# Eight experts in one expert loop: four conditional places for the second block instead of six

## The chip, the cores and the metric

The kernel runs on one core of a Trainium2 chip. The metric is the device time of one execution in microseconds (us), as the median of the runs.

The engines are named as the profile names them: PE multiplies matrices, PEld loads its weights, DVE and ACT work element by element, POOL gathers rows, SP issues most of the transfers. Each engine takes its own instructions strictly in order.

## The reference

The reference is a two-layer encoder trunk. The part around the change is the mixture of experts in the second layer: 512 tokens, each sent to the two best of eight experts.

```
logits = hf @ w_router + b_router
top_logit, top_idx = lax.top_k(logits, 2);  gate = softmax(top_logit)
expert e:  y = (silu(x @ w1[e]) * (x @ w3[e])) @ w2[e]     # 1024 -> 1408 -> 1024
out[token] += gate * y
```

How many tokens an expert gets is known only on the chip.

## The kernel before

**Pieces.** An expert's weights come from HBM as 35 pieces of 128 rows in the order of `SEQ`. Pieces 0 to 7 and 8 to 15 are `w1` and `w3` for hidden columns 0 to 511 and 512 to 1023 (512 KB each). Pieces 16 to 19 are `w2` for the first of these chunks. Pieces 20 to 27 are `w1` and `w3` for the last 384 hidden columns (384 KB each). Pieces 28 to 31 and 32 to 34 are `w2` for the second and third chunk. In the text "piece 31" is the place of a piece in its expert.

**Buffers.** `fetch` (L1289) has SP issue the transfer of a piece into one of 18 raw buffers. `cut` (L1304, L1306) has ACT write the upper half of the number (`whi` or `r_hi`) and DVE the rest (`wlo` or `r_lo`) into a ring of 5; it runs 4 pieces ahead of PE.

**Two blocks of tokens.** `A` takes a piece for the expert's first 128 tokens (the first block): three products of the halves, six matmuls (L1353). `B` takes pieces for the tokens behind 128 (the second block), from the raw buffer, at fp32 (L1357). Whether there is a second block is decided at run time: `B` is a conditional place, with a body for up to 64 rows when the expert has over 160 tokens, a body for up to 32 rows when it has over 128, and nothing otherwise. Every engine with instructions in a body carries the compares and jumps of the place (L1505, L1508; L1502 for the last expert). In this run the first four experts skip their places, the fifth and seventh take the 32-row body and the sixth and eighth the 64-row body.

**Freeing.** A raw buffer is free when the cut and the second block are both done with it. So `refill` stands behind each place: passing the place releases the fetches of the pieces 18 further on, for all pieces that the place covers. In the skipped case PE passes the place without matmuls and signals all the same.

**Steps around a chunk.** `evac` computes silu times the other half (ACT L1368, DVE L1362 or L1369) and `turn` transposes the result for the down projection; for the second block ACT copies the transposed tile `gB` out of the bank `pub` (L1398), and the up projections of the second block write the same bank. Behind piece 28 and 29 `half_T` transposes the next expert's tokens (PE L1326, splits at L163 on ACT and DVE), and behind piece 30 `rows_T` transposes its second block (PE L1313) into the bank that the first `half_T` used. After the last expert `merge` (L1436) adds its output to the tokens.

**Order.** PE, ACT and DVE run in the order in which the code is written here. SP's instructions are placed by the scheduling layer; a body can hold the store of the second block's result on SP (`put`, L1411).

Of the kernel before, what the change touches and what calls it, by code (L numbers as in the profile page):

```python
# [25 lines left out]
NK = 8  # L26
# [3 lines left out]
NE = 8  # L30
# [14 lines left out]
def trunk(ctx, tc, I, out, dbg=None):  # L45
# [1053 lines left out]
    def moe(j, l, N, nxt):  # L1099
# [104 lines left out]
        def token_ids(es, b, ps, whole=True, make=True, count=True):  # L1204
            c = slice(b * 128, (b + 1) * 128)
            for e in es:
                oh_e = ohs[(2 * e + b) % 3]
                if make:
                    for t in range(NT):
                        ts(oh_e[:, t, :], iota256[:, c], posm[:, t, e:e + 1], None, op0=OP.is_equal)  # L1210
                for t in range(NT if count else 0):
                    done = mm(ps[:, (b * NE + e) * 2:(b * NE + e) * 2 + 2], oh_e[:, t, :], tk2[:, t, :],
                              start=(t == 0), stop=(t == NT - 1))
            if count:
                tm.append(done)
            if whole:
                return numbers(es, b, ps)

        def numbers(es, b, ps):
            q = slice(es[0], es[-1] + 1)  # L1220
            nc.vector.tensor_reduce(out=tif[:, b, q], in_=ps[:, 16 * b:16 * b + 16].rearrange("p (e c) -> p e c", c=2)[:, q],
                                    axis=AX.X, op=OP.add)
            return nc.vector.tensor_copy(TI[:, b, q], tif[:, b, q])

        def gather(xg, idx, src=hd):
            return nc.gpsimd.indirect_dma_start(out=xg, out_offset=None, in_=src,  # L1226
                                         in_offset=bass.IndirectOffsetOnAxis(ap=idx, axis=0))
# [30 lines left out]
        SEQ = []  # L1258
# [32 lines left out]
        def fetch_any(n, er=None):  # L1291
            if n < NW:
                fetch(n, er, nc.sync if er is None else nc.gpsimd)
            else:
                nc.sync.dma_start(out=raws[n % NRAW].rearrange("p (a b) -> p a b", a=2), in_=tail[n - NW])
# [12 lines left out]
        def rows_T(xg, he, banks):  # L1308
            n = xg.shape[0]
            per = 512 // n  # L1310
            for h in range(NK // per):
                for k in range(per):
                    done = nc.tensor.transpose(banks[h][:, k * n:(k + 1) * n],  # L1313
                                        xg[:, (per * h + k) * 128:(per * h + k + 1) * 128], ident[0:n, 0:n])
                p3 = banks[h].rearrange("p (k q) -> p k q", k=per)
                if n == 128:
                    split(p3, he[0][:, per * h:per * h + per, :], he[1][:, per * h:per * h + per, :])
                else:
                    act(he, p3, AF.Copy)
            return done  # L1320
# [8 lines left out]
        def quads(m, i):  # L1329
            return m == 32  # L1330
# [33 lines left out]
        def evac(i, m):  # L1364
            fw = FCH[i][1]
            if m == 128:
                src, gated = (tA[1] if i == 2 else tA[i])[:, :fw], tA[i % 2][:, :fw]
                act(src, pa_[2 * (i % 2)][:, :fw], AF.Silu)  # L1368
                (ordered if i == 2 else partial(tt, op=OP.mult))(out=gated, in0=src, in1=pa_[2 * (i % 2) + 1][:, :fw])  # L1369
            else:  # L1370
                n, w_ = (64, fw // 2) if quads(m, i) else (m, fw)
                act(tB[i % 2][64:64 + n, :w_], pub[0:n, :w_], AF.Silu)
                f = ordered if i == 2 and m == 64 else partial(tt, op=OP.mult)
                f(out=tB[i % 2][0:n, :w_], in0=tB[i % 2][64:64 + n, :w_], in1=pub[64:64 + n, :w_])
# [38 lines left out]
        def fold(m):  # L1413
            gather((xa, ye)[m % 2], G.slot[:, m % 2, m // 2:m // 2 + 1], yd)

        def add(m):
            t, i = m // 2, m % 2
            stt(X[t], (xa, ye)[i], G.gate[i][:, t:t + 1], X[t], op0=OP.mult, op1=OP.add)
# [21 lines left out]
        def expert(e, he, hb=None, total=NW + len(tail), base=None, er=None):  # L1440
            base = e * NP if base is None else base
            last = er is None and e == NE - 1
            state = {"a": 0, "b": 0, "cut": 0, "got": 0}

            def refill():
                while state["got"] < state["b" if er is None else "a"]:
                    n = base + state["got"] + NRAW
                    if n < total:
                        fetch_any(n, er)
                    state["got"] += 1  # L1450

            def hook(j):
                if e > 0 or er is not None:
                    return
                if j == 6:
                    rows_T(xb, heB[0], (pub,))
                    gather(xb, TI[0:64, 1, 1:2])
                if 3 <= j < 15:
                    i = j - 1
                    token_ids([i // 2 + 1], i % 2, (pd[0], pdb)[i % 2], whole=False, make=False)  # L1460
                if 2 <= j < 14:
                    token_ids([j // 2 + 1], j % 2, None, whole=False, count=False)
                if j == 14:
                    for b in range(2):
                        numbers(range(2, NE), b, (pd[0], pdb)[b])

            def A(*js):
                for j in js:
                    m = j // 2 - 8
                    if last and j % 2 == 0 and 0 <= m < 2 * NT:  # L1470
                        fold(m)
                    piece(base + j, 0, he)
                    hook(j)
                    state["a"] = j + 1
                    n = base + j + AHEAD
                    if n < total:
                        cut(n)
                        if er is None and 0 < e < 4:
                            next(rest, None)
                    if last and j % 2 and 0 < m <= 2 * NT:  # L1480
                        add(m - 1)
                    if SEQ[j][0] == "u" and SEQ[j][2] == NK - 1:
                        evac(SEQ[j][1], 128)
                    if er is not None:
                        refill()

            def B(lo, hi, before=None):
                if er is not None:
                    return

                def rest_of(m):
                    if before is not None:
                        turn(before, m)
                    for j in range(lo, hi):
                        piece(base + j, 1, hb, m)
                    if SEQ[hi - 1][0] == "u":
                        evac(SEQ[hi - 1][1], m)
                    if hi == NP and not last:
                        put(yd[NE * 128 + e * 64:NE * 128 + e * 64 + 64, :], m, nc.sync)

                if last:
                    with tc.If(cv[e] > 128):  # L1502
                        rest_of(64)
                else:
                    with tc.If(cv[e] > 160) as c:  # L1505
                        rest_of(64)
                    with c.Else():
                        with tc.If(cv[e] > 128):  # L1508
                            rest_of(32)
                state["b"] = hi  # L1510
                refill()

            A(*range(8))
            B(0, 8)
            A(8, 9, 10, 11)
            turn(0, 128)
            A(12, 13, 14, 15)
            B(8, 16, 0)
            A(16, 17, 18)
            turn(1, 128)  # L1520
            A(19)
            B(16, 20, 1)
            A(*range(20, 28))
            B(20, 28)
            A(28)
            if er is None:
                half_T(e + 1, 0)
            A(29)
            if er is None:
                half_T(e + 1, 1)  # L1530
            A(30)
            turn(2, 128)
            if er is None and e + 1 < NE:
                rows_T(xb, heB[(e + 1) % 2], (pa_[2],))
            A(31)
            ahead = er is None and e == NE - 2
            B(28, 35 if ahead else 32, 2)
            A(32, 33, 34)
            if er is None and not last:
                put(yd[e * 128:(e + 1) * 128, :], 128, nc.sync)  # L1540
            if not ahead:
                B(32, 35)
            if last:
                merge()

# [380 lines left out]
```

## Time and profile before

| | us |
|---|---|
| median of 3 runs | 1956.09 (1955.92 to 1959.73) |
| profiled execution, its own time | 1956.71 |
| its span, first to last instruction | 1955.2 |
| PE busy in the span | 1903.8 (97%) |

The times in the profile count from the first instruction. A matmul row of the timeline has the start of a pair and its modelled duration; since matmuls overlap, the distance between the starts of two rows is what a pair costs on PE (0.45 us for a pair of 512 columns, 0.35 for 384).

### The profile page before, as it was taken

To read this page: it belongs to the slowest core of one execution; us is meant where nothing else is said; L and a number is where in the kernel's file an instruction comes from. 1 tells how busy PE (TensorE), PEld (TensorE's weight loads), DVE (VectorE), ACT (ScalarE), POOL (GpSimd) and SP (SyncE) were. 2 spreads that over 40 slices of the span, in tenths; PEclk is the share of its full clock that TensorE was granted. 3 is DMA by queue.
4 is the path that set the end of the run, shared out by engine and by line. 5 is a ranking of instruction groups with operands and counts; after the bars stand their busy time and mean duration, and the time that the engine had idled before them with its cause. 6 is when DMAs were issued, how large, how long until landed. Compare 5 with 4: busy or idle time off the path is not lost. (4 is left out here: it accounts for less than half of the span.)

```text
span 1955.2 us, 27356 instructions
## 1 busy us (share of the span) xinstructions
PE 1903.8 (97%) x9954; PEld 1511.0 (77%) x9954; DVE 1186.8 (61%) x1859; ACT 908.1 (46%) x1349; POOL 332.7 (17%) x632
## 2 busy tenths in 40 slices
PE   7999999999999999999999999999999999999998
PEld 7787777888888888888787677887678877667666
DVE  5867565754333333345767565745899987666674
ACT  5535434333322222254534435333678876556553
POOL 2058220220000000001048320321100000000021
PEclk9999999999999999999999999999999999999999
DMA  5432223234433333432433232335699997756852
GB/s 168 120 116 87 77 91 128 84 95 168 137 97 94 101 97 97 119 91 62 135 114 98 66 92 85 126 96 212 236 370 368 371 357 272 264 202 251 326 160 99
DMA packets 95141, 309.39 MB, mean 158 GB/s; under 512 B 12609, under 2 KB 15681, under 8 KB 94978
## 3 DMA queue, kind: packets, MB, share of 16 engines
q1 hardware_dynamic: 89554, 290.06, 43.5%
q0 software_dynamic: 5280, 16.91, 2.5%
q8 instruction: 100, 1.64, 0.3%
q14 instruction: 63, 0.52, 0.1%
q10 hardware_dynamic: 144, 0.26, 0.0%
HBM read 283.59 MB, written 23.60 MB: 157 GB/s over the span
## 5 line engine op out<-in xcount | busy, mean ns | idle before, releaser
L137 ACT ACTIVATE whi<-wraw 128x1024 fp32r<-128x1024 f32 (+2 forms) x211 | 217.6, 1034 | 483.7 <-PE a L158 265.1
L139 DVE TENSOR_TENSOR wlo<-wraw,whi 128x1024 fp32r<-128x1024 f32 (+2 forms) x211 | 260.0, 1237 | 265.2 <-ACT whi L137 262.9
L157 PE MATMUL a<-hT_hi,whi 128*128 128x512 f32 (+3 forms) x1056 | 412.3, 391 | 1.4 <-ACT hT_hi L163 0.7
L158 PE MATMUL a<-hT_lo,whi 128*128 128x512 f32 (+3 forms) x1056 | 411.5, 390 | 0.8 <-DVE hT_lo L163 0.7
L159 PE MATMUL a<-hT_hi,wlo 128*128 128x512 f32 (+3 forms) x1056 | 411.6, 390 | 0.6 <-DVE wlo L139 0.6
L1306 DVE TENSOR_TENSOR wlo<-raw,whi 128x1024 fp32r<-128x1024 f32 (+1 forms) x198 | 227.8, 1159 | 45.1 <-ACT whi L1304 31.7
L158 PEld LDWEIGHTS a<-hT_lo,whi 128*128 128x128 f32 (+1 forms) x1056 | 197.1, 187 | 42.9 <-issue 2.8
L159 PEld LDWEIGHTS a<-hT_hi,wlo 128*128 128x128 f32 (+1 forms) x1056 | 197.1, 187 | 42.1 <-issue 3.2
L157 PEld LDWEIGHTS a<-hT_hi,whi 128*128 128x128 f32 (+1 forms) x1056 | 196.7, 187 | 42.5 <-issue 1.6
L1304 ACT ACTIVATE whi<-raw 128x1024 fp32r<-128x1024 f32 (+1 forms) x198 | 198.8, 1009 | 48.1 <-PE a L1353 30.4
L157 PE MATMUL a<-whi,hT_hi 128*128 128x256 f32 (+2 forms) x328 | 110.0, 335 | 1.1 <-ACT hT_hi L163 1.1
L159 PE MATMUL a<-whi,hT_lo 128*128 128x256 f32 (+2 forms) x328 | 109.0, 333 | 0.3
L158 PE MATMUL a<-wlo,hT_hi 128*128 128x256 f32 (+2 forms) x328 | 108.6, 331 | 0.0
L664 POOL TENSOR_TENSOR A<-A,t 128x512 f32<-128x512 f32 x48 | 76.4, 1625 | 179.2 <-DVE t L663 179.2
L1353 PE MATMUL a<-whi,heA_hi 128*128 128x512 f32 (+1 forms) x304 | 91.6, 382 | 4.7 <-PEq L1508 1.8
L1353 PE MATMUL a<-wlo,heA_hi 128*128 128x512 f32 (+1 forms) x304 | 88.7, 373 | 0.0
L1353 PE MATMUL a<-whi,heA_lo 128*128 128x512 f32 (+1 forms) x304 | 88.6, 372 | 0.0
L1353 PEld LDWEIGHTS a<-whi,heA_hi 128*128 128x128 f32 x304 | 54.2, 188 | 22.0 <-issue 8.3
L173 POOL TENSOR_SCALAR rs<-ss 128x1 f32<-128x1 f32 x8 | 2.3, 283 | 393.1 <-ACT sq L1773 392.7
L157 PEld LDWEIGHTS a<-whi,hT_hi 128*128 128x128 f32 x328 | 62.5, 191 | 7.0 <-ACT hT_hi L163 1.6
L159 PEld LDWEIGHTS a<-whi,hT_lo 128*128 128x128 f32 x328 | 62.5, 191 | 5.9 <-DVE hT_lo L163 0.9
L1226 POOL DMA_INDIRECT xa<-hd,TI x8 | 12.4, 1553 | 319.0 <-PE a L1326 310.8
(532 smaller groups left out, 3622.5 us busy)
## 6 DMA issues: line engine op xcount, KB each, us to landing
raw<-in_moe_w13a SPq DMA_DIRECT2D x113, 512.0 KB, 7.5
raw<-in_moe_w SPq DMA_DIRECT2D x74, 512.0 KB, 7.9
wraw<-in_w_gate SPq DMA_DIRECT2D x64, 512.0 KB, 3.6
wraw<-in_ffn_w SPq DMA_DIRECT2D x64, 512.0 KB, 3.6
raw<-in_moe_w13b SPq DMA_DIRECT2D x61, 384.0 KB, 7.2
wraw<-in_w_in_T SPq DMA_DIRECT2D x20, 512.0 KB, 3.3
wraw<-in_w_branch SPq DMA_DIRECT2D x16, 512.0 KB, 3.6
wraw<-in_w_o SPq DMA_DIRECT2D x16, 512.0 KB, 3.6
```

Source lines behind the costliest of these rows:

```text
L137: act(hi[:, :n], raw[:, :n], AF.Copy)
L139: tt(out=lo[:, :n], in0=raw[:, :n], in1=hi[:, :n].bitcast(F), op=OP.subtract)
L157: mm(o, a[0], b[0], start=start, stop=False)
L158: mm(o, a[0], b[1], start=False, stop=False)
L159: mm(o, a[1], b[0], start=False, stop=stop)
L173: gts(out=r[:, :n], in0=ss, scalar1=1.0 / dim, scalar2=EPS, op0=OP.mult, op1=OP.add)
L664: gtt(out=A[m], in0=A[m], in1=g[m], op=OP.add)
L1226: return nc.gpsimd.indirect_dma_start(out=xg, out_offset=None, in_=src, in_offset=bass.IndirectOffsetOnAxis(ap=idx, axis=0))
L1304: act(hi[:, :w], raw[:, :w], AF.Copy)
L1306: return tt(out=lo[:, :w], in0=raw[:, :w], in1=hi[:, :w].bitcast(F), op=OP.subtract)
L1353: mm(dst[x][:, :w_], st[sa][:, k, :], w[:, cs[x]], start=first and q == 0, stop=last and q == 2)
```

## The change

Pieces 8 to 19 of the second block run in one body, at the place that stood behind piece 19, and pieces 28 to 34 in one body behind piece 31 (the seventh expert had this already). The place behind piece 15 and the one behind piece 34 are gone. The transposes of the first and second chunk move with them: the first into the body of 8 to 19, the second into the body of 20 to 27. The evacuation of an up projection now stands in the middle of a body.

```diff
@@ -1493,8 +1493,8 @@
                     for j in range(lo, hi):
                         piece(base + j, 1, hb, m)
-                    if SEQ[hi - 1][0] == "u":
-                        evac(SEQ[hi - 1][1], m)
+                        if SEQ[j][0] == "u" and SEQ[j][2] == NK - 1:
+                            evac(SEQ[j][1], m)
                     if hi == NP and not last:
                         put(yd[NE * 128 + e * 64:NE * 128 + e * 64 + 64, :], m, nc.sync)
@@ -1514,14 +1514,12 @@
             B(0, 8)
             A(8, 9, 10, 11)
             turn(0, 128)
-            A(12, 13, 14, 15)
-            B(8, 16, 0)
-            A(16, 17, 18)
+            A(12, 13, 14, 15, 16, 17, 18)
             turn(1, 128)
             A(19)
-            B(16, 20, 1)
+            B(8, 20, 0)
             A(*range(20, 28))
-            B(20, 28)
+            B(20, 28, 1)
             A(28)
...
             A(31)
-            ahead = er is None and e == NE - 2
-            B(28, 35 if ahead else 32, 2)
+            B(28, 35, 2)
             A(32, 33, 34)
             if er is None and not last:
                 put(yd[e * 128:(e + 1) * 128, :], 128, nc.sync)
-            if not ahead:
-                B(32, 35)
             if last:
                 merge()
```

On SP, in the second expert, the place behind piece 15 stood in the middle of the fetches of pieces 26 to 34; now one place (behind piece 19) does what two did (rows cut from the difference; raw buffers by number, those shown carry `w2` pieces).

```order
 L1289 DMA raw_11661<-in_moe_w 128x1024
-L1505 COMPARE_AND_BRANCH
-L1505 UNCONDITIONAL_BRANCH
-L1508 COMPARE_AND_BRANCH
-L1508 UNCONDITIONAL_BRANCH x2
 L1289 DMA raw_11662<-in_moe_w 128x1024
 L1289 DMA raw_11663<-in_moe_w 128x1024
 L1289 DMA raw_11664<-in_moe_w 128x1024
 L1289 DMA raw_11665<-in_moe_w 128x1024
+L1505 COMPARE_AND_BRANCH
+L1505 UNCONDITIONAL_BRANCH
+L1508 COMPARE_AND_BRANCH
```

The order of the fetches among themselves is the same. The branch moved back on SP by four fetches; when a fetch may go is set by PE's signal for its raw buffer.

On PE, in the first expert, the place behind piece 27 (64-row body): `cst,ut` are the transposes of the second chunk into `pub` (tile `b`), the 64x384 rows are pieces 20 and 21, which write `pub` too.

```order
 L1353 MATMUL a<-r_hi,heA_lo 128x384 x2
 L1505 COMPARE_AND_BRANCH
+L1393 MATMUL b<-cst,ut 128x64 x4
 L1357 MATMUL b<-raw_11228,yh 64x384 x2
 L1357 MATMUL b<-raw_11229,yh 64x384 x2
```

The transposes moved from the body before the down projection into this one, directly ahead of the pieces that reuse their bank.

On PE, at the end of the last expert: the `a` and `b` rows at L1353 are its last first-block piece, L1502 its second-block place, and L1436 the first matmuls of `merge`.

```order
 L1353 MATMUL b<-wlo,gA_hi 128x512 x2
 L1353 MATMUL b<-whi,gA_lo 128x512 x2
-L1502 COMPARE_AND_BRANCH
-L1357 MATMUL b<-raw_11233,gB_11680 64x512 x2
-L1357 MATMUL b<-wraw,gB_11680 64x512 x4
-L1502 UNCONDITIONAL_BRANCH x2
 L1436 MATMUL a<-heA_hi,Sel 128x512
 L1436 MATMUL a<-heA_lo,Sel 128x512
```

The second block's last three pieces, which stood between the last first-block piece and `merge`, are now ahead of piece 32.

## Rows read from the trace of the kernel before

**Rows 1.** Fourth, fifth expert: us; PE, PEld, DVE, ACT, POOL busy (count); clock; DMA.

```profile
1547.28:1597.88 50.60, 49.70 (x238) 40.76 (x238) 45.28 (x46) 40.39 (x46) 2.98 (x2) 1.00 0.96 369
1597.88:1663.68 65.80, 65.43 (x524) 49.86 (x525) 48.05 (x50) 42.59 (x54) 2.54 (x2) 1.00 0.77 282
```

**Rows 2.** Timeline of PE, fourth expert: start, duration, instruction, tiles, shapes, count.

```profile
1569.57 0.61 PE L1353 MATMUL a<-whi,heA_lo 128*128 128x512 f32 x2
1570.34 0.71 PE L1353 MATMUL b<-whi,gA_hi 128*128 128x512 f32 x2
1570.88 0.62 PE L1353 MATMUL b<-wlo,gA_hi 128*128 128x512 f32 x2
1571.34 0.62 PE L1353 MATMUL b<-whi,gA_lo 128*128 128x512 f32 x2
...
1576.66 0.59 PE L1353 MATMUL a<-whi,heA_hi 128*128 128x384 f32 x2
...
1590.93 0.70 PE L1313 MATMUL a<-cst,xb 64*128 64x64 f32 x8
```

**Rows 3.** Sequencer instructions of line 1508: PE's compares, ns minimum, median and maximum.

```profile
L1508 PEldq COMPARE_BRANCH  x46: 65/207/1210, 1401.9 to 1804.1; - x46
```

**Rows 4.** Timeline of SP, fourth expert, fetches of pieces 26 to 32.

```profile
1570.31 0.80 SPq L1289 DMA_DIRECT2D raw<-in_moe_w13b  x2
...
1573.29 1.32 SPq L1289 DMA_DIRECT2D raw<-in_moe_w  x2
```

**Rows 5.** Issue to landing: fourth expert's pieces 28 and 31, third expert's 28.

```profile
raw<-in_moe_w SPq DMA_DIRECT2D x1, 512.0 KB, 5.8
...
raw<-in_moe_w SPq DMA_DIRECT2D x1, 512.0 KB, 7.5
...
wraw<-in_moe_w SPq DMA_DIRECT2D x1, 512.0 KB, 6.3
```

**Rows 6.** Timeline of ACT, fourth expert: silu, cut of piece 32, first token split.

```profile
1585.20 0.47 ACT L1368 ACTIVATE ut<-a 128x384 f32<-128x384 f32 x1
1585.88 1.06 ACT L1304 ACTIVATE r_hi<-raw 128x1024 fp32r<-128x1024 f32 x1 [0.20 <-ACTq L1508]
1587.49 0.60 ACT L163 ACTIVATE heA_hi<-a 128x512 fp32r<-128x512 f32 x1 [0.55 <-PE a L1326]
```

**Rows 7.** Timeline of DVE: the gated product, cut of piece 32, token split.

```profile
1586.76 0.61 DVE L1362 TENSOR_TENSOR ut<-ut,a 128x256 f32<-128x256 f32 x2
1587.60 1.23 DVE L1306 TENSOR_TENSOR r_lo<-raw,r_hi 128x1024 fp32r<-128x1024 f32 x1 [0.23 <-DVEq L1508]
1588.75 0.68 DVE L163 TENSOR_TENSOR heA_lo<-a,heA_hi 128x512 fp32r<-128x512 f32 x1
```

**Rows 8.** PE, fifth expert (32-row body): the two places around pieces 16 to 19.

```profile
1624.11 0.34 PE L1393 MATMUL b<-cst,ut 64*128 64x64 f32 x2
1624.81 1.93 PE L1357 MATMUL b<-raw,yh 128*32 128x256 f32 x32 [0.37 <-ACT gB L1398]
...
1633.99 0.62 PE L1353 MATMUL b<-whi,gA_lo 128*128 128x512 f32 x2
1634.55 0.33 PE L1393 MATMUL b<-cst,ut 64*128 64x64 f32 x2
1634.81 1.93 PE L1357 MATMUL b<-raw,gB 128*32 128x256 f32 x32
```

**Rows 9.** At the merge: ACT's splits, PE's second block and fifth matmul, DVE's split.

```profile
1887.48 1.08 ACT L163 ACTIVATE heA_hi<-b 128x512 fp32r<-128x512 f32 x2 [6.08 <-PE b L1353]
...
1888.50 1.89 PE L1357 MATMUL b<-wraw,gB 128*64 128x512 f32 x8
...
1892.15 0.40 PE L1436 MATMUL a<-heA_hi,Sel 128*128 128x512 f32 x1
...
1891.07 0.69 DVE L163 TENSOR_TENSOR heA_lo<-b,heA_hi 128x512 fp32r<-128x512 f32 x1 [1.67 <-ACT heA_hi L163]
```

**Rows 10.** Waits of SP, 1640 to 1815 us, its stores in a body.

```profile
SPq L1411 <- ACT yb L1409: 44.7, 3, 20.3
```

## The prediction

> **What bounds the kernel now.** I read the busy time by stretch first, one stretch per expert. In the fourth expert, which skips its second block, PE is busy for 49.70 of 50.60 us at a granted clock of 1.00, and at the same time the DMA engines are busy for 0.96 of it [rows 1]. So PE sets the pace there, and the transfers have almost nothing to spare. In the fifth, which takes its bodies, PE is busy for 65.43 of 65.80 us and the DMA share is 0.77 [rows 1]. The reader is to see two kinds of expert: four that skip, where any late transfer may show, and four that take a body, where PE alone counts.
>
> Then PE's timeline at a place [rows 2]. Pairs of matmuls start 0.46 us apart (1570.88 to 1571.34). Across the skipped place the distance is 0.77 (1569.57 to 1570.34), 0.31 more; the next pair takes 0.54 instead of 0.46. A skipped place costs PE 0.31 + 0.08 = 0.4 us.
>
> Last I followed SP's fetches beside PE. The fetch of piece 26, the first that the place behind piece 15 holds back, is issued at 1570.31 [rows 4], just as PE gets past that place (1570.34) [rows 2]. So passing the place is what releases it.
>
> **The change part by part.** *Places removed in the four skipping experts.* Two each, behind pieces 15 and 34, so 8 x 0.4 = 3.2 us less PE time. Nothing lies beside this, since PE is the busy engine: I count all of it.
>
> [...] The row of compares has 207 ns as its median on PE [rows 3], and the gap on PE is 0.31, so I stay with the gap.
>
> *The fetches of pieces 26 to 33.* These now wait for the place behind piece 19. In the fourth expert that is 1576.66 [rows 2] instead of 1570.34: 6.3 us later relative to PE's work. What covers that? Piece 31 is issued at 1573.29 [rows 4] and lands 7.5 us later [rows 5], at 1580.8, which is 10.5 us after the first fetch of its batch. If the batch restarts in the same manner, it lands at 1576.7 + 10.5 = 1587.2 on the old clock. Behind it ACT and DVE work in order, with durations from [rows 6, 7]:
>
> ACT cuts piece 31 (1.06, as for piece 32), to 1588.3; silu, 0.47, to 1588.8; cuts piece 32, to 1589.9; splits the first half of the next expert's tokens, 0.60, to 1590.5. DVE's part of piece 31 (1.23) ends at 1589.5, the gated product (0.61) at 1590.1, its part of piece 32 at 1591.4, its part of the token split (0.68) at 1592.1. PE's transposes at L1313 reuse the bank that this split reads; they start at 1590.93 today [rows 2], when the split is long over (1588.75 + 0.68 = 1589.4 [rows 7]). They would start 1.2 us later.
>
> So the 6.3 us are covered but for 1.2 us in the fourth expert. In the third, piece 28 lands 6.3 us after its issue, in the fourth 5.8 [rows 5], and piece 31 goes with it: about 1.7 us there. I take 1.5 us as the mean of the four skipping experts: 4 x 1.5 = 6.0 us more. The bounds: nothing, if the batch starts with 1.5 us less delay than today; 2.5 us each, if it starts 1 us worse than in the fourth expert and DVE has small extra work besides. With the saving that is -3.2 to +6.8 us for these experts, and +2.8 as the value taken. Can the transfers catch up, at a share of 0.96? The pause before piece 26 grows only in the first expert. After that the whole stream runs later by about this much and ends just as the next place is passed, so it costs once per expert and does not grow.
>
> *The four experts that take a body.* In the 32-row body of pieces 8 to 15, PE's transposes start at 1624.11 and the matmuls at 1624.81, since they write the bank that ACT is still copying from: 0.70 us. In the body of 16 to 19, which writes another bank, it is 0.26 [rows 8]. The second transpose now stands before pieces 20 to 27, which write the bank: a new wait of 0.44 us in each of four experts, more in a 64-row body, so I take 0.5, 2.0 in all. Against it, joining two bodies saves a switch: 0.1 on entering (0.56 from 1633.99 to 1634.55 instead of 0.46), and I take the same again for leaving and for the first pair behind it, 0.3. There are seven such switches (the seventh expert loses only one place): 2.1. The two cancel.
>
> The fetches in these experts have more cover: at a DMA share of 0.77 [rows 1] nothing queues long, and the bodies give PE work while they land. I put this at nothing; if the cover is gone it is the 1.2 us from above in the fifth, at most.
>
> *SP's store in a body.* SP waits up to 20.3 us for the result of the second block before it stores it [rows 10], and fetches stand queued behind. The store now stands earlier among the fetches, but the result is ready earlier too, by the first block's pieces 32 to 34 (3 x 1.4 = 4.1 us). Nothing, with 0 to 1 us each in two experts as bounds.
>
> *The merge.* In the last expert pieces 32 to 34 of the second block ran while ACT and DVE split the first block's result. ACT begins these splits at 1887.48, two take 1.08, and DVE's last takes 0.69 behind a third on ACT [rows 9]. Today PE reaches its fifth matmul of the merge at 1892.15, 4.7 us after 1887.48. With the second block already done, the chain is 1.08 + 0.5 on ACT, 0.1, 0.69 on DVE, then 0.4 on PE: 2.8. The three second-block pieces come earlier instead: twelve matmuls at 1.89 us for eight [rows 9] make 2.8, and I take 2.6, since the row's end overlaps what follows. 2.8 + 2.6 - 4.7 = 0.7 us more.
>
> **The sum.** -3.2 + 6.0 + 0.0 + 0.7 = +3.5 us. The profiled execution took 1956.71, so 1960.2; the median of the runs is 0.6 below it, so 1956.09 + 3.5 = 1959.6.
>
> **The rivals.** *A cheap restart, faster than before.* If the batch behind the later place lands 1.5 us sooner than its model, PE never waits at L1313, and 3.2 us are saved for 0.7: 1953.6. For it speaks that DMA might work off a longer run of fetches in a better stream; against it that today's restart, in much the same situation, took those 10.5 us for six pieces, 2.88 MB, which at the mean of 369 GB/s [rows 1] would take 7.8.
>
> *The transfers become the bound, clearly slower.* At a share of 0.96 [rows 1], a stream that runs 6 us later leaves little slack for cuts in the whole next expert. It decides as soon as piece 31 lands more than about 11.3 us after the first fetch: each us beyond that is a us on PE. At 2.5 us per expert: 4 x 2.5 - 3.2 + 0.7 = +7.5, 1963.6. For it speaks the fuller queue; against it that the queue empties just before each place.
>
> *The longer jump.* The longest of PE's 46 compares took 1.21 us against a median of 0.21 [rows 3]. The skipped body grows from eight pieces to twelve; a jump that stalls 1 us and is not hidden, once in each skipping expert, adds 4.0: 1963.6. The gaps on PE did not show that long compare as more than the usual 0.3 us, which speaks against. [...]
>
> *The places cost more than their gap.* If compares also delay ACT and DVE, 16 places less on each engine could be worth 5 us: 1951. The gap rows show no such thing.
>
> **How the numbers follow.** No change here means within 0.2%, 3.9 us, which is about what a measurement of this kernel can tell. The forecast, +3.5, gets 0.47; with 1.5 us either way it lies within the bound in two cases of three (0.32) and above it in one (0.15). The cheap restart gets 0.17, nearly all within. The transfers as the bound get 0.22 and the longer jump 0.07, both beyond. The places that cost more get 0.07, faster. Slower: 0.15 + 0.22 + 0.07 = 0.44; the same: 0.32 + 0.17 = 0.49; faster: 0.07. Range: from the cheap restart, 1953.5, to a little beyond the transfers as the bound, 1964.5. The likeliest case alone is 1958.1 to 1961.1.
>
> **What would show it.** Right, if the gaps behind pieces 15 and 34 are gone in the skipping experts, if the fetch of piece 26 goes out as PE passes the place behind piece 19, if PE stands before L1313 or a piece between 28 and 31 for about 1.5 us in each of them, waiting for DVE's split or a cut, if PE waits for `gB` in eight bodies instead of four, and if the merge shows about 1 us of wait. Wrong, if there is no wait at pieces 28 to 32, if the waits spread over the next expert's pieces, or if a gap at a place is longer than 0.4 us.

## The result: slower by 0.53%, more than forecast

The changed kernel takes 1968.24 us (median of 5 runs, 1965.85 to 1969.12), beside 1956.61 for the kernel before in the same session. The medians differ by 11.6 us. The ratio on record, over all runs, is 1.0053 with a 95% interval of 1.0042 to 1.0065, which is 10.4 us. The forecast was +3.5 us (1959.6) in a range up to 1964.5. The sign of the sum was right, its size was not, and the time lies outside the range.

### Where the time went

The start of each expert's first matmul pair in the two profiled executions (spans 1955.2 and 1967.6 us) splits the difference. The eighth ends at the fifth matmul of `merge`.

| expert | body | before, us | after, us | difference |
|---|---|---|---|---|
| first to fourth | skipped | 58.3, 50.6, 50.8, 50.6 | 59.1, 51.5, 52.2, 53.7 | +0.8, +0.9, +1.4, +3.1 |
| fifth | 32 rows | 65.8 | 67.1 | +1.3 |
| sixth | 64 rows | 80.4 | 80.2 | -0.3 |
| seventh | 32 rows | 67.6 | 72.7 | +5.1 |
| eighth | 64 rows, `merge` | 80.5 | 81.4 | +1.0 |

A row has the time from an expert's start to the next one's. The rows sum to +13.4 us. The first expert starts 1.0 us earlier, and what follows takes 63.0 us in both. The windows of the fourth, fifth and seventh expert of the changed kernel answer to [rows 1] (columns as there):

```profile
1549.41:1603.10 53.69, 50.97 (x239) 41.77 (x237) 44.98 (x47) 39.41 (x46) 2.87 (x2) 0.97 0.94 364
1603.10:1670.23 67.13, 64.81 (x525) 50.63 (x524) 46.87 (x49) 42.50 (x55) 2.55 (x2) 1.00 0.72 272
1750.40:1823.11 72.71, 66.63 (x525) 50.98 (x524) 48.61 (x50) 42.94 (x55) 0.00 (x0) 0.98 0.66 249
```

PE now stands idle in the fourth expert (50.97 busy of 53.69, where it was 49.70 of 50.60), and the granted clock, 1.00 before, is 0.97 and 0.98 over the fourth and the seventh. PE's waits from the first expert to the end, the largest sums (who waited for what, us in total, times, longest), name the places. Before:

```profile
PE a L1353 <- PEq L1508: 1.8, 5, 1.1
PE a L1353 <- DVEq L1730: 1.8, 1, 1.8
PE b L1357 <- ACT gB L1398: 1.7, 4, 0.5
```

After:

```profile
PE b L1357 <- ACT gB L1398: 6.5, 7, 3.9
PE a L1313 <- DVE heA_lo L163: 5.4, 4, 1.7
PE b L1357 <- issue: 2.0, 1, 2.0
PE a L1353 <- DVEq L1725: 1.8, 1, 1.8
PE a L1353 <- PEq L1508: 1.3, 2, 1.2
PE a L1436 <- DVE heA_lo L163: 0.7, 2, 0.5
PE a L1436 <- ACT heA_hi L163: 0.6, 1, 0.6
```

The second row of after is the wait that was forecast, once in each skipping expert. The first and the third are where the forecast fell short: `gB`, at most 0.5 us before and 0.37 in [rows 8], and forecast at 0.5 in each of four more bodies, costs 3.9 us once and 2.0 us once more. The latter is the "issue" row, in the fifth expert: the profile names no releaser, but PE starts as ACT's copy of `gB` ends.

```profile
1651.62 0.27 ACT L1398 ACTIVATE gB<-b 128x128 f32<-128x128 f32 x1
1651.98 1.34 PE L1357 MATMUL b<-raw,yh 128*32 128x192 f32 x27 [1.96 <-issue]
```

The 1.8 us at L1730 (L1725 after) are the start of the eighth expert, alike in both kernels.

The reader can follow the first kind of loss in the fourth expert, on PE (timeline: start, duration, instruction, idle time before it in brackets):

```profile
1592.76 0.55 PE L1393 MATMUL a<-cst,ut 128*128 128x128 f32 x3 [0.42 <-DVE ut L1362]
1595.01 0.71 PE L1313 MATMUL a<-cst,xb 64*128 64x64 f32 x8 [1.70 <-DVE heA_lo L163]
...
1596.80 1.06 PE L1353 MATMUL b<-whi,gA_lo 128*128 128x512 f32 x2
1598.01 1.19 PE L1353 MATMUL b<-r_hi,gA_hi 128*128 128x512 f32 x2
1599.00 1.05 PE L1353 MATMUL b<-r_lo,gA_hi 128*128 128x512 f32 x2
1599.85 0.69 PE L1353 MATMUL b<-r_hi,gA_lo 128*128 128x512 f32 x2
1600.38 0.62 PE L1353 MATMUL b<-whi,gA_hi 128*128 128x512 f32 x2
```

After the two waits the pairs come 0.99 and 0.85 us apart (1598.01 to 1599.85) instead of 0.46. The windows of the same stretch (granted clock third from the end) say why:

```profile
1592.50:1595.00 2.50, 0.55 (x3) 0.34 (x3) 2.27 (x5) 2.50 (x5) 0.68 (x1) 1.00 1.03 419
1595.00:1597.50 2.50, 2.50 (x14) 1.83 (x14) 2.50 (x3) 2.42 (x4) 0.90 (x1) 0.81 1.03 419
1597.50:1600.00 2.50, 2.35 (x6) 1.64 (x6) 2.50 (x4) 1.06 (x1) 0.00 (x0) 0.51 1.03 415
1600.00:1602.50 2.50, 2.50 (x13) 2.05 (x12) 1.33 (x2) 1.62 (x2) 0.00 (x0) 1.00 1.04 321
```

PE had worked 0.55 us of 2.50 at a granted clock of 1.00; then the clock fell to 0.81 and 0.51 over the next two stretches and came back to 1.00. From 1596.23 to 1600.38 five pairs took 4.15 us; at 0.454 each and 0.4 for the skipped place they would take 2.7. So the lower clock cost some 1.5 us there.

The second kind of loss, in the seventh expert, starts with idle transfers. The DMA row over 1770 to 1800 us (40 equal slices, busy share in tenths):

```profile
DMA  9999999721000000000000079975999999999999
```

SP's fetches (timeline, columns as for PE):

```profile
1786.40 0.80 SPq L1289 DMA_DIRECT2D raw<-in_moe_w13b  x2
1787.31 1.86 SPq L1289 DMA_DIRECT2D raw<-in_moe_w  x4
```

For some 10 us next to nothing is moved, since pieces 26 and up are fetched only once the joined body has used the buffers. ACT, which works in order, then takes the cuts as they land:

```profile
1794.34 1.06 ACT L1304 ACTIVATE whi<-raw 128x1024 fp32r<-128x1024 f32 x1 [1.60 <-DMA raw<-in_moe_w]
1795.56 1.06 ACT L1304 ACTIVATE whi<-raw 128x1024 fp32r<-128x1024 f32 x1 [0.16 <-DMA raw<-in_moe_w]
1798.36 1.06 ACT L1304 ACTIVATE whi<-raw 128x1024 fp32r<-128x1024 f32 x1 [1.74 <-DMA raw<-in_moe_w]
1799.58 1.06 ACT L1304 ACTIVATE whi<-raw 128x1024 fp32r<-128x1024 f32 x1 [0.16 <-DMA raw<-in_moe_w]
1800.54 0.47 ACT L1368 ACTIVATE ut<-a 128x384 f32<-128x384 f32 x1
1800.91 0.27 ACT L1398 ACTIVATE gB<-b 128x128 f32<-128x128 f32 x1
```

The copy of `gB` stands behind the cuts of pieces 28 to 31: ACT stands idle until 1798.36 for the third of these cuts, while the transposes that the copy takes (0.33 us from 1796.99, below) are done. PE, with pieces 20 to 27 in their buffers, waits for it because they write the bank `pub`:

```profile
1796.99 0.33 PE L1393 MATMUL b<-cst,ut 64*128 64x64 f32 x2
1801.23 4.49 PE L1357 MATMUL b<-raw,yh 128*32 128x192 f32 x64 [3.91 <-ACT gB L1398]
```

The same 64 matmuls took 2.81 us in the kernel before. The 4.49 here, 1.7 more, fall in a stretch of granted clock 0.66. Before (timeline) and after (window):

```profile
1791.50 2.81 PE L1357 MATMUL b<-raw,yh 128*32 128x192 f32 x64
1801.00:1806.00 5.00, 4.77 (x66) 3.19 (x67) 1.51 (x3) 0.36 (x3) 0.00 (x0) 0.66 0.65 238
```

### The profile page after: what moved, and what is told of

Same layout as the page of the kernel before. It is cut to its first block, busy times and chain, and to the rows that moved or that the text cites. A ratio compares the mean times of both kernels' runs of the same rounds, so it can differ in the third digit from the quotient of the medians.

```text
span 1967.6 us, 27167 instructions
## 1 busy us (share of the span) xinstructions
PE 1903.2 (97%) x9954; PEld 1514.1 (77%) x9954; DVE 1185.2 (60%) x1859; ACT 904.9 (46%) x1349; POOL 327.3 (17%) x632
## 5 line engine op out<-in xcount | busy, mean ns | idle before, releaser
L1353 PE MATMUL a<-whi,heA_hi 128*128 128x512 f32 (+1 forms) x304 | 90.9, 380 | 4.0 <-DVEq L1725 1.8
L1353 PE MATMUL a<-wlo,heA_hi 128*128 128x512 f32 (+1 forms) x304 | 88.6, 372 | 0.0
L1353 PE MATMUL a<-whi,heA_lo 128*128 128x512 f32 (+1 forms) x304 | 88.5, 372 | 0.0
L1353 PEld LDWEIGHTS a<-whi,heA_hi 128*128 128x128 f32 x304 | 54.6, 188 | 18.9 <-issue 6.8
L158 PEld LDWEIGHTS a<-wlo,hT_hi 128*128 128x128 f32 x328 | 62.5, 191 | 4.7
```

The lines of the kernel that those rows point to most:

```text
L158: mm(o, a[0], b[1], start=False, stop=False)
L1353: mm(dst[x][:, :w_], st[sa][:, k, :], w[:, cs[x]], start=first and q == 0, stop=last and q == 2)
```

## The experiments

The theory after the comparison: all of the loss comes from the later release of the fetches of pieces 26 to 34, by a late chain on ACT and DVE in the skipping experts, by `gB` queued behind late cuts in the experts with a 32-row body, and by the clock that falls after such waits. The rivals: the joined bodies or the moved transposes cost it by themselves, the last body carries it, or PE's pieces are late as such. Each kernel ran in 5 rounds beside the kernel before, except the last one told, which ran once. The ratios are those on record, over all runs of a kernel and of the kernel before in the same session; times by expert are of one profiled execution each.

**One half of the change each.** `only_28_34` is the kernel before with `B(28, 35, 2)` in all experts:

```diff
-            ahead = er is None and e == NE - 2
-            B(28, 35 if ahead else 32, 2)
+            B(28, 35, 2)
...
-            if not ahead:
-                B(32, 35)
```

> The kernel before with one half of the change: pieces 28 to 34 in one body in every expert; pieces 8 to 15 and 16 to 19 stay in two places. Theory (late release): the place behind piece 15 still releases the fetches of pieces 26 to 33, so nothing new is waited for. Four skipped places less at 0.4 us make -1.6, three joined bodies at 0.3 make -0.9, the merge costs +1.0: about -1.5, so 1955.1 us against 1956.6. Rival (the long last body or the merge carries the loss): 1962 or more.

1955.96 us, ratio 0.9991 (0.9982 to 1.000). The skipping experts two to four take 50.2 us each instead of 50.6 to 50.8, the eighth, with the merge, 81.4 instead of 80.5. A skipped place is worth its 0.4 us, and the joined last body brings no net loss, though the merge costs the eighth expert 0.9. `only_8_19` is the other half, the changed kernel with pieces 28 to 34 in two places as before:

> The changed kernel with pieces 28 to 32 and 32 to 34 in two places as before, so only pieces 8 to 19 are joined, behind piece 19. Theory (late release): all of the loss is here. Against the changed kernel the merge gives back 1.0 us and four skipped places and three switches cost 2.5: about 1969.5 us. Rival (the last body carries the loss): 1960 or less.

1971.38 us, ratio 1.0069 (1.0054 to 1.0085). The six runs lie between 1966.4 and 1974.5, so its distance to the changed kernel is not clear. All of the loss is in joining pieces 8 to 19 behind piece 19.

**The joined body at an earlier place.** `early_8_19`:

```diff
-            A(12, 13, 14, 15, 16, 17, 18)
+            A(12, 13, 14, 15)
+            B(8, 20, 0)
+            A(16, 17, 18)
             turn(1, 128)
             A(19)
-            B(8, 20, 0)
```

> The changed kernel with the one body of pieces 8 to 19 standing behind piece 15 instead of behind piece 19: as many places and bodies as in the changed kernel, but the fetches of pieces 26 and up are released as early as in the kernel before. Theory (late release): no wait for the token split at the transposes behind piece 30, no long wait for gB, no fall of the clock; eight skipped places less make -3.2, seven switches -2.1, four short gB waits +2.0, the merge +1.0: about -2.3, 1954.3 us. Rival (the joined body or the moved transposes cost it by themselves): like the changed kernel, 1966 to 1969.

1958.85 us, ratio 1.0010 (1.0001 to 1.0019). Of the changed kernel's 11.6 us nearly all are gone, with the same bodies: the wait at L1313 no longer shows, `gB` costs at most 0.5 us, and the clock is 1.00 in every expert. But it is no gain of 2.3 us either. A new wait stands right at the place, in the second expert (timeline of PE):

```profile
1468.52 0.61 PE L1353 MATMUL a<-whi,heA_lo 128*128 128x512 f32 x2
1470.43 0.70 PE L1353 MATMUL b<-whi,gA_hi 128*128 128x512 f32 x2 [1.30 <-PEq L1508]
```

PE's sequencer spent 4972 ns in one compare that began at 1465.30 (4635 ns at 1566.36 in the fourth). The matmul pair behind it could have started at 1469.1, 3.8 us after the compare began, so only the rest shows. In 1464 to 1472 us the DMA queue for instructions moved two blocks:

```profile
q8 instruction: 2, 0.03, 1.9%
```

The first of them was moved from 1467.95 to 1468.91, within the compare, which ended at 1470.27. This is the stall that the forecast's rival of the longer jump had in view. The changed kernel hides it: its longest compares in these experts are 1847 and 1197 ns, and only the second is at this place.

**The transposes of the second chunk back ahead of the late cuts.** `turn_back` is the changed kernel with

```diff
+                    if hi == 20:
+                        turn(1, m)
                     if hi == NP and not last:
...
-            B(20, 28, 1)
+            B(20, 28)
```

> The changed kernel with the second block's transposes of the second chunk moved to the end of the body of pieces 8 to 19, so that ACT copies gB before the late cuts of pieces 28 to 31 and not behind them; the fetches stay late. Theory (in the experts with a body the loss is gB's copy queued behind late cuts): the waits for gB go (2.0 us in the fifth expert, 3.9 and about 1.7 of lowered clock in the seventh, 0.5 each in the sixth and eighth), the waits of the skipping experts stay: 1959 to 1961 us. Rival (the pieces themselves are late for PE): the waits come back at the first block's pieces 28 to 31 in the fifth and seventh, 1966 to 1968.

1963.30 us, ratio 1.0025 (1.0014 to 1.0036), 2 us above the expected band. The experts with a body confirm the theory. The fifth and the seventh:

```profile
1604.99:1670.09 65.10, 64.73 (x526) 50.24 (x524) 46.70 (x50) 42.52 (x55) 2.53 (x2) 1.00 0.75 292
1749.68:1816.75 67.07, 64.90 (x526) 50.08 (x524) 48.63 (x50) 43.03 (x55) 0.00 (x0) 1.00 0.71 273
```

They take 2.0 and 5.6 us less than in the changed kernel and are 0.7 and 0.5 shorter than before [rows 1], although the fetch of piece 26 goes out nearly as late as in the changed kernel (35.6 us after the start of either expert; there 36.0, in the kernel before 29.3 and 29.4). So what cost them was the copy of `gB` behind late cuts on ACT, and a joined body by itself is a gain. The band was missed elsewhere: the skipping experts kept their waits at L1313 (5.2 us in four) and had 1.1 and 0.9 us of new waits for DVE beside them, one fell to a clock of 0.97 behind a wait of 1.50 us, and the 63.0 us behind the experts became 64.6. There the clock fell to half at 1897.7 (0.92 over the 64.6 us, where the changed kernel has 0.95 over its 63.0), behind two short waits in the merge (0.57 and 0.45 us), which the changed kernel has too (0.55 and 0.46) without a fall behind them.

**Another bank for the waiting transposes.** `turn_back_pub` changes one more word:

```diff
-                rows_T(xb, heB[(e + 1) % 2], (pa_[2],))
+                rows_T(xb, heB[(e + 1) % 2], (pub,))
```

> The kernel turn_back (changed kernel, second transposes back in the body of pieces 8 to 19) with the transposes of the next expert's second block (L1313) written into the bank pub instead of the bank that the token split still reads. Theory (the skipping experts lose only at that bank: the late split is waited for, PE's own pieces are not late): the four waits at L1313, 5.2 us, go, and no wait of that size takes their place: 1956 to 1958 us. Rival (the transfers are late as such): PE waits as long at the cuts of pieces 31 and 32, 1961 to 1964.

1961.63 us, ratio 1.0025 (1.0014 to 1.0036). My theory of the bank falls. The waits at L1313 are gone and others of nearly the same sum stand behind the next piece, at piece 32 (waits of PE in the skipping experts and the start of the fifth):

```profile
PE b L1353 <- DVE gA_lo L163: 2.6, 3, 0.9
PE b L1353 <- ACT gA_hi L163: 2.0, 2, 1.5
PE b L1353 <- DVE wlo L1306: 0.5, 2, 0.2
```

The rival had the size, though not the tile: PE waits for the split of `gA` for piece 32, which ACT and DVE reach late because the cuts ahead of it are late. The bank was only where the delay first surfaced.

**How late is too late.** `mid_8_19` puts the body behind piece 17, with the transposes at its end as in `turn_back` and the last expert's pieces 32 to 34 apart as before:

```diff
-            A(12, 13, 14, 15, 16, 17, 18)
+            A(12, 13, 14, 15, 16, 17)
+            B(8, 20, 0)
+            A(18)
...
-            B(28, 35, 2)
+            B(28, 32 if last else 35, 2)
...
             if last:
+                B(32, 35)
                 merge()
```

> The joined body of pieces 8 to 19 behind piece 17, between the two places tried: second transposes at its end, pieces 32 to 34 of the last expert apart as before. The fetches of pieces 26 and up are then released 2.8 us later than in the kernel before, not 6.3 us. Theory (6.3 us less a wait of 1.1 to 1.7 us says that some 4.8 us are covered, and the long compares on PE come from instruction fetches behind a full DMA queue): no wait at L1313, compares under 3 us, hence hidden; eight skipped places make -3.2, the joined bodies -2: about 1952 us. Rival 1 (the long jump itself costs 4 to 5 us as behind piece 15): 1954 to 1956. Rival 2 (any later release costs): waits at L1313 stay, 1956 or more.

1952.36 us, ratio 0.9971 (0.9962 to 0.9981): faster than both kernels, as forecast. No wait at L1313. The compares were not under 3 us, though: 3044 ns in the second expert, hidden, and 4688 ns in the fourth, where 1.1 us shows. That they come from fetches of instructions was a guess of mine, which no run shows. So rival 1 holds in part. The same kernel with the body behind piece 16 and behind piece 18:

> The kernel mid_8_19 with the joined body behind piece 16 instead of 17: fetches released 1.4 us later than in the kernel before. Theory (up to some 4.8 us of delay is covered): no wait at L1313, skipping experts at 49.8 us apart from compares, 1952 to 1953 us. Rival (an earlier release helps by itself): below 1951.

> The kernel mid_8_19 with the joined body behind piece 18: fetches released 4.2 us later than in the kernel before, 2.1 us earlier than in the changed kernel. Theory (some 4.8 us are covered, by the waits of 1.1 to 1.7 us out of 6.3): waits at L1313 under 0.3 us each, 1952 to 1954 us. Rival (the cost grows with each us of delay from the start): some 0.7 us in each skipping expert, 1955 to 1957.

Behind 16: 1952.59 us, ratio 0.9974 (0.9963 to 0.9985), experts two to four at 49.8 us each. Behind 18: 1953.13 us, ratio 0.9973 (0.9962 to 0.9984), but these experts take 50.3, 50.7 and 49.8 us. Two small waits are all that the list of waits shows there:

```profile
PE a L1393 <- DVE ut L1369: 0.6, 1, 0.6
PE a L1313 <- DVE heA_lo L163: 0.4, 1, 0.4
```

Both are in the third expert. A release 1.4 or 2.8 us later costs nothing, one of 4.2 us costs 0 to 0.9 us in an expert, one of 6.3 us costs the waits of the changed kernel. By these executions the cover, the delay that costs PE nothing, ends between 2.8 and 4.2 us, sooner than the 4.8 that I had expected. The times of the runs do not tell 2.8 from 4.2 (ratios 0.9971 and 0.9973).

**The jump.** `one_body` is `mid_8_19` with only the 64-row body at the place of pieces 8 to 19 in the first four experts:

```diff
-                if last:
+                if last or (lo == 8 and hi == 20 and e < 4):
                     with tc.If(cv[e] > 128):
```

> The kernel mid_8_19 in which the first four experts have only the 64-row body at the place of pieces 8 to 19 (one compare instead of two, half the instructions to jump over; they skip it in any case). Theory (the compares of 3.0 and 4.7 us at that place are jumps over a long stretch of instructions): compares under 2 us there, no gap of 1.1 us in the fourth expert, one compare less in four experts: 1950 to 1952 us. Rival (the long compares come from somewhere else, as from the transfers beside them): they stay at 3 us or more, 1951.5 to 1953.

1950.89 us, ratio 0.9958 (0.9944 to 0.9971), the lowest of all, though its interval overlaps with that of `mid_8_19`. The compares at that place take at most 0.35 us (one of 1219 ns is left, behind piece 31 and hidden), and the wait of 1.1 us is gone too:

```profile
1445.12:1494.95 49.83, 49.23 (x238) 40.92 (x237) 46.74 (x76) 41.35 (x48) 2.63 (x2) 1.00 0.97 376
1494.95:1544.77 49.82, 49.22 (x239) 40.93 (x238) 46.97 (x67) 41.12 (x47) 2.96 (x2) 1.00 0.95 376
1544.77:1594.58 49.81, 49.21 (x239) 40.91 (x237) 45.23 (x46) 40.22 (x46) 2.36 (x2) 1.00 0.96 373
```

With two bodies of twelve pieces to jump over, behind piece 15, 16 or 17, the compare took 3.0 to 5.0 us in the second and the fourth expert and at most 0.35 in the first and the third; with one body it is short in all four. The edit also takes out a compare and shifts the code behind it, so the length of the jump is not told apart from where the code falls. The DMA share of these experts (0.95 to 0.97) is that of `mid_8_19` (0.96 and 0.97), so a full stream of transfers does not make the long compare by itself. This form suits experts that skip; one with up to 32 rows would take the larger body, which no run shows.

**The merge.** `last_apart` is `only_28_34` with the last expert as before:

```diff
-            B(28, 35, 2)
+            B(28, 32 if last else 35, 2)
...
             if last:
+                B(32, 35)
                 merge()
```

> The kernel only_28_34 with pieces 28 to 32 and 32 to 34 of the last expert in two places as before. Theory (the merge is slower by 1 us because its splits on ACT and DVE have nothing beside them): the waits of the merge go, the last expert takes 80.5 us instead of 81.4, about 1 us less than only_28_34, so 1954.5 to 1955.5. Rival (it is the joined body): no difference to only_28_34.

1954.36 us, ratio 0.9988 (0.9979 to 0.9997). The waits for `heA_hi` and `heA_lo` in the merge (0.6 and 0.7 us) shrink to one of 0.2, and the last expert takes 80.5 us instead of 81.4. The intervals of the two kernels overlap, so the 0.9 us rest on the profiled executions.

**The clock by itself.** `stall` makes PE wait in the kernel before:

```diff
+            for _ in range({1: 2, 2: 5, 3: 9}.get(e, 0) if er is None else 0):
+                act(pa_[2], pa_[2], AF.Copy)
             if er is None and e + 1 < NE:
                 rows_T(xb, heB[(e + 1) % 2], (pa_[2],))
```

> The kernel before with extra copies on ACT, which PE has to wait for at the transposes behind piece 30: two copies in the second expert (PE idle about 1.3 us), five in the third (about 2.7), nine in the fourth (about 4.5). Theory (the granted clock falls after PE has stood idle long enough, and then costs by itself): the clock stays at 1.00 in the second expert and falls behind the wait in the fourth, where the next pairs take twice as long for some us, so the fourth loses some 2 us more than its wait. Rival (the falls seen in the changed kernel came from elsewhere): the clock stays at 1.00 in all three, each loses its wait alone.

One execution: 1975.6 us. The waits became longer than meant, 2.91, 3.52 and 5.98 us, so no expert had a short one. All three fell (second to fourth expert):

```profile
1446.53:1501.54 55.01, 51.20 (x238) 41.65 (x238) 47.83 (x78) 42.83 (x50) 1.85 (x2) 0.97 0.98 365
1501.54:1557.21 55.67, 51.14 (x238) 41.88 (x238) 47.29 (x65) 44.13 (x52) 2.72 (x2) 0.97 0.91 340
1557.21:1616.76 59.55, 52.68 (x238) 42.83 (x238) 45.30 (x46) 45.51 (x55) 2.73 (x2) 0.91 0.87 328
```

Against [rows 1] and the table above they lose 4.4, 4.9 and 9.0 us, that is 1.5, 1.4 and 3.0 more than the waits, and no other wait of theirs grew. That such a wait of PE brings the fall with it, and what it costs, is shown; from what length on is not.

## Why the prediction was wrong

**Right: the mechanism in the skipping experts.** The forecast said that fetch 26 goes out as PE passes the place behind piece 19 (it does in the fourth expert: 1578.28 on SP, 1578.31 on PE) and that PE then waits at L1313 for the split on DVE, 1.2 to 1.7 us in each, 6.0 in all. It waits 1.09, 1.33, 1.26 and 1.70 us, 5.4 in all. From the landing of piece 31 on, the chain took what was reckoned (1590.05, ACT's cut, to 1594.95, the split's end: 4.9 us, as forecast). The landing itself was later: ACT began the cut 11.1, 10.7, 11.1 and 11.8 us after the first fetch in the four experts, where 10.5 was reckoned. The saving of 0.4 us a place was right too (`only_28_34`).

**Mis-sized there.** These four experts were to lose 2.8 us and lost 6.2. The late chain also shows at other tiles (0.4 us twice before transposes, some of 0.2), about 1.5 us together; the fall of the clock in the fourth adds another 1.5. With 5.4 for the wait and -3.2 for the places that makes 5.2; the last 1.0 us is not accounted for. The sum of the prediction had no term for the clock.

**The step that failed** is "The fetches in these experts have more cover: ... I put this at nothing; if the cover is gone it is the 1.2 us from above in the fifth, at most." With the moved transposes, priced at 0.5 us each, they cost 2.0 us in the fifth and 3.9 in the seventh, and the clock 1.7 more: 7.6 us, where the sum had 1.0. The fifth to seventh expert together were forecast at nothing and lost 6.1, most of what the forecast missed. I had looked at the DMA share and at PE's own pieces, and both were indeed no problem. What I left out is the third in the chain: ACT holds the cuts of pieces 28 to 31 and `gB` in one queue, with the cuts first since they run four pieces ahead. I had priced the moved transposes at the copy alone, 0.5 us, without asking what stands ahead of the copy on its engine. It took both changes: with early fetches (`early_8_19`) the moved transposes cost 0.39 to 0.47 us each, as forecast, and with late fetches but the transposes back ahead of the cuts (`turn_back`) the 2.0 and 5.6 us are gone. The size in the seventh is partly chance: there ACT began the cut of piece 31 13.2 us after the first fetch, in `only_8_19`, with the same order, 11.8, and that wait was 2.5 us.

**Joined bodies are a gain.** I let seven switches (2.1) and the new waits (2.0) cancel. Without these waits the fifth and seventh expert are 0.7 and 0.5 us shorter than before (`turn_back`), so the switches were mis-sized little.

**The merge** was forecast at +0.7. The eighth expert takes 0.9 us more in `only_28_34`, with one switch saved that the forecast counts elsewhere at 0.3, so it was mis-sized by some 0.5; its waits are those of the chain behind [rows 9].

**The rivals.** Two of them had 1963.6, nearest in time. The transfers as the bound were to decide once piece 31 lands more than 11.3 us after the first fetch; the cut began past that in the fourth expert alone. The stream was full while it caught up (a share of 1.03 to 1.04 from 1592.5 to 1602.5), but `mid_8_19` moves the same pieces at 0.96 to 0.97 without such a wait, so what costs is the late release. The stall that the longer jump was to bring did come on this program (a compare of 4.97 us in `early_8_19`) and is hidden in the changed kernel; it takes 1.0 to 1.3 us of PE's time where nothing else delays PE. That the length of the jump makes it was not shown (`one_body`).

**The signs.** Those named for a right forecast all came: PE waits for `gB` eight times instead of four, and the merge shows 1.3 us of wait. They asked whether the waits are there, not how long the late ones are, so they could not tell the forecast from what happened.

## What to carry to other kernels

Before you merge two synchronisation points, ask for each buffer that the earlier one freed how much later its refill starts, and follow the late data through every in-order engine, not only to the matmul that uses it: what is queued behind it may be what somebody else waits for. When an instruction is moved, price what stands ahead of it on its engine as well as its own duration. A place that can be moved by small steps (here one piece, 1.4 us) is worth trying between the ends: the cover was some 3 us, and within it joining the bodies was a gain.

## What the runs showed of the hardware

A wait of PE can cost more than itself (1.4 to 3.0 us more in `stall`). Waits of 1.09 to 1.36 us left the granted clock of their expert at 1.00, and so did one of 1.49 (`turn_back_pub`), the 1.8 at the start of the eighth expert in every run, and the 1.96 in the fifth expert of the changed kernel. One of 1.50 us (`turn_back`), 1.70 with 0.42 before it, and all of 2.5 us and more were followed by some us at half the clock (0.50 over a stretch in `stall`, 0.51 in the changed kernel); so were two of 0.57 and 0.45 us in the merge of `turn_back` and again, with 0.55 and 0.45, in that of `turn_back_pub` (0.92 from the merge to the end in both), while the same two in the changed kernel were not (0.95, as in the kernel before). The length of the last wait alone does not decide it; what does stays open. Behind the longest, 5.98 us, pairs of matmuls came 0.85 to 1.2 us apart until 1613.7, 6.8 us after PE had started again (timeline of PE in `stall`):

```profile
1606.88 1.11 PE L1313 MATMUL a<-cst,xb 64*128 64x64 f32 x8 [5.98 <-ACT a L1534]
1607.92 1.22 PE L1353 MATMUL b<-whi,gA_hi 128*128 128x512 f32 x2
...
1612.84 1.03 PE L1353 MATMUL b<-r_hi,gA_lo 128*128 128x512 f32 x2
1613.69 0.64 PE L1353 MATMUL b<-whi,gA_hi 128*128 128x512 f32 x2
```

A compare at a skipped place took PE's sequencer 0.21 us mostly [rows 3] and up to 4.97 where it jumps over two bodies of twelve pieces; with one such body, at most 0.35. The long ones end at a like distance from another event: the 25 compares over 0.5 us at these places in the thirteen profiles all ended 1.36 to 1.51 us after a block of 16 KB on the instruction queue had been moved (in the second expert of `early_8_19` the block at 1468.91, the compare at 1470.27). In the changed kernel such a block had been moved at 1533.69 and the compare of 1847 ns ended at 1535.13. What a block held, and whether the compare waited for it, no run shows.
